# Attention: the exponentials of every third key tile are summed by accumulating transfers instead of VectorE adds

## The chip, the core and the metric

The kernel runs on one core of one Trainium2 chip. The core has five engines that run side by side, each with an instruction queue of its own that is worked off in order: TensorE (PE, matrix products), VectorE (DVE), ScalarE (ACT), GpSimd (POOL) and SyncE (SP, which only issues transfers). Transfers (DMAs) are issued by SP, by ScalarE, and in the changed kernel by GpSimd too; all run on the core's 16 DMA engines. The metric is the device time of one execution in microseconds; smaller is better.

## What is computed

One layer of a diffusion backbone over 2048 latent tokens with a prefix of 256 context tokens, d_model 1024, all in float32. The change touches the attention only:

```python
def attend(q, k, v):
    s = jnp.einsum('bkgqd,bknd->bkgqn', q, k, preferred_element_type=jnp.float32)
    p = jax.nn.softmax(s, axis=-1).astype(v.dtype)
    return jnp.einsum('bkgqn,bknd->bkgqd', p, v)
...
k_all = jnp.concatenate([k_c, k_x], axis=2)      # 256 context keys + 2048 latent keys
v_all = jnp.concatenate([v_c, v_x], axis=2)
attn_x = merge_heads(attend_blocked(q_x, k_all, v_all))
gm_x = gmlp_spatial(jax.nn.gelu(u_x), jax.nn.gelu(vg_x), gm_norm_g[l], gm_ws[l], gm_bs[l])
x = x + g1 * branch_merge(attn_x, gm_x, ga_x, gb_x, w_br_attn[l], w_br_gm[l], w_out[l])
h2 = modulate(x, norm2_g[l], sh2, sc2)
x = x + g2 * sq_relu_mlp(h2, w_ff1[l], w_ff2[l])
```

There are 8 query heads of 64 elements over 2 key/value heads. The softmax needs, for each query, the sum of the exponentials over all 2304 keys. That sum is the subject of the change.

## The kernel before

The kernel runs through four stages, one after the other: the input projections with norms and gates (to about 735 us), attention (about 735 to 1340 us), the merge of the branches with the output projection (to about 1700 us), and the MLP.

Attention is cut into 16 units: 4 query blocks of 512 queries, times 4 pairs of heads. A unit goes over the 2304 keys in 18 key tiles of 128 keys, two tiles in each of 9 cycles (`CYCLES`). The function `attend` writes out the order by hand. In cycle c of a unit stand, in this order:

- `maxima` (L2433), twice: TensorE computes scores of a coming unit once more (L2447) into one of three banks `m`, and VectorE reduces each bank to its maximum per query (L2457, L2452); the maxima later serve as the reference of the exponentials. Up to cycle 5 this is for the next unit, from cycle 6 on for the one after it.
- `scores` for the two key tiles of the cycle: TensorE computes them transposed, keys on partitions (L2504), with the reference added in the first two tiles by a product with `ones`; ScalarE takes the exponential of a whole 128x1024 tile (two heads of 512 queries, L2510). Tiles with an even number go to buffers `p2` (8 slots), those with an odd number to buffers `t4` (8 slots); the profile calls them `p` and `t`.
- `values` for the two tiles of the cycle before: TensorE multiplies them with v into the bank `o` (L2518).
- `gather` for the same two tiles: the exponentials are summed over the key tiles, elementwise, in two running sums. Key tiles 2, 5, 8, 11 and 14 (`ON_VECTOR`) go into VectorE's sum (L2535, one instruction of 128x1024 a tile); the other thirteen go into GpSimd's (L2538, two instructions of 128x512 a tile). The first tile of each sum is kept as it is, so VectorE has 4 adds in a unit and GpSimd 12 tiles, 24 adds. The running sums live in buffers `ac` (4 slots), two for each unit. The last unit has a list of its own (`LAST_ON_VECTOR`).
- `join` (L2549) for the unit before: VectorE adds its sum to GpSimd's (L2553), the first head in cycle 2 and the second in cycle 4. In cycle 5 `sums` (L2556) lets TensorE add up the 128 partitions of the result with a product by `ones`.
- other work in single cycles: in cycles 1 and 7 a step of the modulation weights on VectorE (L424, L428), in cycle 1 the inverse of the sums (L2579), in cycle 6 `reference` and `leading`, which turn the maxima of the next unit into rows and let SP write them into its tile `top` with eight small transfers (L2482); and in the last three to four units, in cycles 1, 4 and 7, a step of the next stage's inputs on VectorE (L1552, L1559).

The order within the queues of TensorE and VectorE is held as written (`self.fixed` in `build` and `order`). A slot of a buffer is taken again when its last reader has finished.

Of the kernel before, what the change touches and what calls it, by code (L numbers as in the profile page):

```python
# [14 lines left out]
ALU = mybir.AluOpType  # L15
# [54 lines left out]
PAIR = 2  # L70
CYCLES = NKT // PAIR
AHEAD = 6
ON_VECTOR = (2, 5, 8, 11, 14)
LAST_ON_VECTOR = (2, 4, 7, 8, 9, 12, 13, 14, 15)

OPENING = """
# [24 lines left out]
class Kern:  # L101
# [1324 lines left out]
    def attend(self, units, late, mod, key_loads):  # L1426
        self.psum({"s": 2, "m": 3, "o": 1})
        self.nc.gpsimd.memset(self.rg["q"], 0.0)
        begin = self.here()
        n = len(units)  # L1430
        pend = []

        def ordered(work):
            at = self.here()
            work()
            self.loads.append(range(at, self.here()))

        for i, u in enumerate(units):
            at = lambda k: units[k] if 0 <= k < n else None
            nxt, far, old, older = at(i + 1), at(i + 2), at(i - 1), at(i - 2)  # L1440
            u.banks()
            for c in range(CYCLES):
                step = nxt if c < AHEAD else far
                if c == 0 and far:
                    far.load()
                if step:
                    step.maxima(1)
                group = range(PAIR * c, PAIR * (c + 1))
                for j in group:
                    u.scores(j)  # L1450
                if step:
                    step.maxima(1)
                owner = u if c else old
                for j in pend:
                    owner.values(j)
                if c == 0:
                    if old:
                        old.leave()
                    u.o = self.bank([TB], tag="o")
                if c == 5 and old:  # L1460
                    old.sums()
                if c == AHEAD and nxt:
                    nxt.reference()
                    ordered(nxt.leading)
                for j in pend:
                    owner.gather(j)
                if i and c in (1, 7):
                    next(mod, None)
                if c == 1 and older:
                    older.inverse()  # L1470
                if c in (2, 4) and old:
                    old.join(c // 4)
                if i == 0:
                    next(key_loads, None)
                if i + c / CYCLES > n - 4 and c % 3 == 1:
                    ordered(lambda: next(late, None))
                pend = list(group)
        for _ in mod:
            pass
        owner = units[-1]  # L1480
        for j in pend:
            owner.values(j)
            owner.gather(j)
        units[-2].inverse()
        total = [self.sb("raw", [TB]) for _ in range(2)]
        for h in range(2):
            units[-1].join(h, total)
        self.fixed.append(range(begin, self.here()))
# [924 lines left out]
class Unit:  # L2413
# [109 lines left out]
    def gather(self, j):  # L2523
        k, nc = self.k, self.nc
        pt = self.pts.pop(j)
        e = j in (LAST_ON_VECTOR if self.last else ON_VECTOR)
        old = self.acc.get(e)
        if old is None:
            self.acc[e] = pt
            return  # L2530
        if e not in self.own:
            self.own.add(e)
            self.acc[e] = k.sb("ac", [2, TB])
        if e:
            nc.vector.tensor_tensor(out=self.acc[e], in0=old, in1=pt, op=ALU.add)  # L2535
        else:
            for h in range(2):
                nc.gpsimd.tensor_tensor(  # L2538
                    out=self.acc[e][:, h], in0=old[:, h], in1=pt[:, h], op=ALU.add
                )  # L2540
# [92 lines left out]
```

## Time and profile before

| | |
|---|---|
| median of 3 runs | 2974.29 us (2971.73 to 2974.46) |
| profiled execution | 2974.45 us, span of its instructions 2972.7 us |
| granted TensorE clock, mean | 0.993 |
| busy over the whole span: TensorE, VectorE, ScalarE, GpSimd | 98%, 69%, 47%, 21% |
| attention, 735 to 1340 us: TensorE, VectorE, ScalarE, GpSimd busy | 595.2, 509.7, 306.5, 554.0 us of 605 |
| DMA engines busy in attention, mean | 13% |

The shares of the whole span mix four stages: GpSimd has nearly all of its work in attention. In the rows of the profile, `ac<-ac,p` is an add of a `p` tile to a running sum, and "<-DVE ts L2457" behind a row means that the wait before it ended with that VectorE instruction. Rows of the form "start us, us, engine line op" come in order of time. Idle time of an engine costs nothing unless an engine that sets the end waits for it.

### The profile page before, as it was taken

What the parts mean: (1) busy time and instruction counts of PE and PEld (TensorE: products, weight loads), DVE (VectorE), ACT (ScalarE), POOL (GpSimd) and SP (SyncE); (2) the same over time, 40 slices, a digit from 0 to 9 for tenths busy, and PEclk for the clock granted to TensorE, in tenths of its full rate; (3) what the DMA queues carried; (4) which work ended last, traced back from release to release, by engine and by line L of the source; (5) the groups of instructions that cost most, each with busy time, mean ns of one, the idle gap of its engine ahead of it and who ended that gap; (6) DMA issues with size and microseconds to landing.
All of it is one profiled execution on the core that took longest, in us unless ns stands there. A gap on an engine that the chain in (4) does not pass through costs nothing. (4 is left out here: it accounts for less than half of the span.)

```text
span 2972.7 us, 39185 instructions
## 1 busy us (share of the span) xinstructions
PE 2898.6 (98%) x14126; PEld 2186.8 (74%) x14126; DVE 2058.5 (69%) x3018; ACT 1391.8 (47%) x1993; POOL 633.0 (21%) x444
## 2 busy tenths in 40 slices
PE   8999999999999999999999999999999999999999
PEld 7878787776554545447888878887888888888887
DVE  6866487766888898866555687775766766654555
ACT  6545865553554554553222354444453444444442
POOL 0000000000999999972221100000000000000000
PEclk9999999999999999999999999999999999999999
DMA  8688967777110100117766578888766444447654
GB/s 309 189 302 284 311 205 226 252 247 222 56 36 27 37 30 28 45 45 239 214 205 202 152 255 305 299 294 307 258 219 229 168 141 152 152 175 260 218 211 151
DMA packets 392947, 569.09 MB, mean 191 GB/s; under 512 B 39264, under 2 KB 194576, under 8 KB 392752
## 3 DMA queue, kind: packets, MB, share of 16 engines
q1 hardware_dynamic: 380448, 545.87, 54.8%
q10 hardware_dynamic: 12304, 20.71, 1.9%
q8 instruction: 111, 1.82, 0.3%
q14 instruction: 84, 0.69, 0.1%
HBM read 383.82 MB, written 182.58 MB: 191 GB/s over the span
## 5 line engine op out<-in xcount | busy, mean ns | idle before, releaser
L2457 DVE TENSOR_REDUCE ts<-m 128x1 f32<-128x512 f32 x472 | 300.2, 682 | 54.8 <-PE m L2447 52.8
L2061 DVE TENSOR_TENSOR b<-b,b 128x1024 fp32r<-128x1024 f32 x170 | 200.8, 1222 | 135.4 <-ACT b L2060 134.5
L2538 POOL TENSOR_TENSOR ac<-ac,p 128x512 f32<-128x512 f32 x160 | 266.3, 1686 | 42.7 <-ACT p L2510 42.5
L2060 ACT CAST b<-b 128x1024 fp32r<-128x1024 f32 x170 | 170.7, 1051 | 223.2 <-PE b L1945 100.1
L1944 PE MATMUL b<-b,b 128*128 128x512 f32 x680 | 265.1, 390 | 3.0 <-DVE b L2061 3.0
L1943 PE MATMUL b<-b,b 128*128 128x512 f32 x680 | 266.0, 391 | 1.7 <-DVE f L2082 1.5
L1945 PE MATMUL b<-b,b 128*128 128x512 f32 x680 | 264.7, 389 | 0.0
L2510 ACT ACTIVATE p<-s 128x1024 f32<-128x1024 f32 x149 | 152.4, 1026 | 223.7 <-PE s L2504 204.0
L2538 POOL TENSOR_TENSOR ac<-ac,t 128x512 f32<-128x512 f32 x184 | 251.3, 1393 | 6.1 <-ACT t L2510 6.1
L2504 PE MATMUL s<-h,h 64*128 64x512 f32 x1728 | 227.8, 391 | 0.0
L2504 PEld LDWEIGHTS s<-h,h 64*128 64x128 f32 x1728 | 161.3, 184 | 39.6 <-ACT t L2510 4.1
L1944 PE MATMUL b<-hb,b 128*128 128x512 f32 x446 | 174.1, 390 | 0.0
L1953 DVE TENSOR_TENSOR f<-f,b 128x512 f32<-128x512 f32 x160 | 109.3, 683 | 81.0 <-issue 46.9
L1945 PE MATMUL b<-hb,b 128*128 128x512 f32 x415 | 161.8, 391 | 0.0
L1943 PE MATMUL b<-hb,b 128*128 128x512 f32 x415 | 161.7, 390 | 0.0
L2518 PE MATMUL o<-p,h 128*64 128x512 f32 x596 | 160.8, 621 | 0.0
L1944 PEld LDWEIGHTS b<-b,b 128*128 128x128 f32 x680 | 127.7, 188 | 31.3 <-DVE b L2061 4.6
L1943 PEld LDWEIGHTS b<-b,b 128*128 128x128 f32 x680 | 127.6, 188 | 29.6 <-ACT b L2060 2.3
L2447 PEld LDWEIGHTS m<-h,h 64*128 64x128 f32 x584 | 60.4, 184 | 119.6 <-DVE ts L2457 95.9
L1945 PEld LDWEIGHTS b<-b,b 128*128 128x128 f32 x680 | 127.6, 188 | 26.4
L2518 PE MATMUL o<-t,h 128*64 128x512 f32 x556 | 144.7, 599 | 0.0
L2510 ACT ACTIVATE t<-s 128x1024 f32<-128x1024 f32 x139 | 141.4, 1018 | 0.0
(468 smaller groups left out, 7058.5 us busy)
## 6 DMA issues: line engine op xcount, KB each, us to landing
ao_d<-f SPq DMA_DIRECT2D x224, 256.0 KB
f<-in_w_ff SPq DMA_DIRECT2D x48, 1024.0 KB
b<-ao_d SPq DMA_DIRECT2D x85, 512.0 KB
b<-w2o_d SPq DMA_DIRECT2D x85, 512.0 KB
w2o_d<-f SPq DMA_DIRECT2D x112, 256.0 KB
f<-in_w_in SPq DMA_DIRECT2D x38, 512.0 KB
f<-x_d SPq DMA_DIRECT2D x64, 256.0 KB
hb<-ao_d SPq DMA_DIRECT2D x54, 256.0 KB
```

What stands on the lines that cost most here:

```text
L1943: mm(ps, wh, hh, start=start and k == 0, stop=False, skip_group_check=True)
L1944: mm(ps, wh, hl, start=False, stop=False, skip_group_check=True)
L1945: mm(ps, wl, hh, start=False, stop=k == len(w) - 1, skip_group_check=True)
L1953: nc.vector.tensor_tensor(out=out, in0=in0, in1=in1, op=op)
L2060: nc.scalar.copy(h, f32(l))
L2061: nc.vector.tensor_tensor(out=l, in0=f32(l), in1=f32(h), op=ALU.subtract)
L2447: nc.tensor.matmul(out, self.q[0][rows, tok], key[rows], start=True, stop=True)
L2457: nc.vector.tensor_reduce(out=self.mx[:, t, h, c : c + 1], in_=ps[h], axis=AX.X, op=ALU.max)
L2504: nc.tensor.matmul(s[:, h], w[rows], x[rows], start=j < PAIR and n == 0, stop=n == len(terms) - 1, skip_group_check=True,)
L2510: nc.scalar.activation(pt, s, AF.Exp)
L2518: nc.tensor.matmul(self.o[h * HD : (h + 1) * HD, :], k.V[c][:, i, self.kv * HD : (self.kv + 1) * HD], pt[:, h], start=j == 0, stop=j == NK ...
L2538: nc.gpsimd.tensor_tensor(out=self.acc[e][:, h], in0=old[:, h], in1=pt[:, h], op=ALU.add)
```

## The change

```diff
@@ -70,7 +70,7 @@
 AHEAD = 6
-ON_VECTOR = (2, 5, 8, 11, 14)
+SUMMED = 3
 LAST_ON_VECTOR = (2, 4, 7, 8, 9, 12, 13, 14, 15)
@@ -1468,8 +1468,8 @@
                 if c == 1 and older:
                     older.inverse()
-                if c in (2, 4) and old:
-                    old.join(c // 4)
+                if c in (3, 4) and old:
+                    old.join(c - 3)
@@ -2523,10 +2523,13 @@
         pt = self.pts.pop(j)
-        e = j in (LAST_ON_VECTOR if self.last else ON_VECTOR)
+        e = j in LAST_ON_VECTOR if self.last else j % SUMMED == SUMMED - 1
         old = self.acc.get(e)
         if old is None:
             self.acc[e] = pt
+            return
+        if e and not self.last:
+            nc.gpsimd.dma_start(out=old, in_=pt, accum_op=ALU.add)
             return
```

In each of the first 15 units, key tiles 2, 5, 8, 11, 14 and now 17 form the second sum. Tile 2's buffer is that sum, and tiles 5, 8, 11, 14 and 17 are added to it by five transfers from SBUF to SBUF that accumulate (each 128 rows of 4 KB, 512 KB). GpSimd issues them, in its own queue between its adds. GpSimd's own sum has one tile less (17). VectorE has no add of a key tile any more; it joins the two sums, in cycles 3 and 4 of the next unit instead of 2 and 4. Only one `ac` buffer is needed for a unit. The last unit stays as it was.

GpSimd's queue in the second unit, from key tile 3 on, before. `t_1398` is tile 3, `p_1407` tile 4, `p_1413` and `t_1414` are tiles 6 and 7, `t_1421` is tile 9; `Activation` is a wait for ScalarE, `Pool` one for GpSimd's own earlier work:

```order
L2538 TENSOR_TENSOR ac_7701<-ac_7701,t_1398_7689 128x512 [waits Activation_49,Pool_49]
L2538 TENSOR_TENSOR ac_7701<-ac_7701,t_1398_7689 128x512 [waits Pool_49]
L2538 TENSOR_TENSOR ac_7701<-ac_7701,p_1407_7722 128x512 [waits Activation_49,Pool_49]
L2538 TENSOR_TENSOR ac_7701<-ac_7701,p_1407_7722 128x512 [waits Pool_49]
L2538 TENSOR_TENSOR ac_7701<-ac_7701,p_1413_7757 128x512 [waits Activation_49,Pool_49]
L2538 TENSOR_TENSOR ac_7701<-ac_7701,p_1413_7757 128x512 [waits Pool_49]
L2538 TENSOR_TENSOR ac_7701<-ac_7701,t_1414_7765 128x512 [waits Activation_49,Pool_49]
L2538 TENSOR_TENSOR ac_7701<-ac_7701,t_1414_7765 128x512 [waits Pool_49]
L2538 TENSOR_TENSOR ac_7701<-ac_7701,t_1421_7801 128x512 [waits Activation_49,Pool_49]
L2538 TENSOR_TENSOR ac_7701<-ac_7701,t_1421_7801 128x512 [waits Pool_49]
```

The same place in the changed kernel (the numbers in the names differ, the tiles are the same; `p_1396` is tile 2, `t_1407` tile 5, `p_1418` tile 8; `DMASW` is a wait for an earlier transfer that GpSimd issued):

```order
L2541 TENSOR_TENSOR ac_7699<-ac_7699,t_1397_7687 128x512 [waits Activation_49,Pool_49]
L2541 TENSOR_TENSOR ac_7699<-ac_7699,t_1397_7687 128x512 [waits Pool_49]
L2541 TENSOR_TENSOR ac_7699<-ac_7699,p_1406_7720 128x512 [waits Activation_49,Pool_49]
L2541 TENSOR_TENSOR ac_7699<-ac_7699,p_1406_7720 128x512 [waits Pool_49]
L2532 DMA p_1396_7679<-t_1407_7728 128x1024 [waits PE_49,Activation_49]
L2541 TENSOR_TENSOR ac_7699<-ac_7699,p_1412_7754 128x512 [waits Activation_49,Pool_49]
L2541 TENSOR_TENSOR ac_7699<-ac_7699,p_1412_7754 128x512 [waits Pool_49]
L2541 TENSOR_TENSOR ac_7699<-ac_7699,t_1413_7762 128x512 [waits Activation_49,Pool_49]
L2541 TENSOR_TENSOR ac_7699<-ac_7699,t_1413_7762 128x512 [waits Pool_49]
L2532 DMA p_1396_7679<-p_1418_7790 128x1024 [waits DMASW5_49,Activation_49]
L2541 TENSOR_TENSOR ac_7699<-ac_7699,t_1419_7798 128x512 [waits Activation_49,Pool_49]
L2541 TENSOR_TENSOR ac_7699<-ac_7699,t_1419_7798 128x512 [waits Pool_49]
```

A transfer now stands after every two tiles of adds, and from the second on it waits for the one before it.

VectorE's queue around the two joins of a unit, before. `ac_8068` is GpSimd's sum and `ac_8145` VectorE's of the unit before; `p_1536` and `t_1546` are tiles 2 and 5 of the running unit, `m` the banks of the maxima:

```order
L2553 TENSOR_TENSOR ac_8068<-ac_8068,ac_8145 128x512 [waits DVE_49,Pool_49]
L2457 TENSOR_REDUCE ts_7991<-m_8476 128x1 [waits PE_49]
L2457 TENSOR_REDUCE ts_7991<-m_8477 128x1 [waits PE_49]
L2457 TENSOR_REDUCE ts_7991<-m_8498 128x1 [waits PE_49]
L2457 TENSOR_REDUCE ts_7991<-m_8499 128x1 [waits PE_49]
L2535 TENSOR_TENSOR ac_8510<-p_1536_8413,t_1546_8461 128x1024 [waits Activation_49]
L2457 TENSOR_REDUCE ts_7991<-m_8512 128x1 [waits PE_49]
L2457 TENSOR_REDUCE ts_7991<-m_8513 128x1 [waits PE_49]
L2457 TENSOR_REDUCE ts_7991<-m_8534 128x1 [waits PE_49]
L2457 TENSOR_REDUCE ts_7991<-m_8535 128x1 [waits PE_49]
L2553 TENSOR_TENSOR ac_8068<-ac_8068,ac_8145 128x512 [waits Pool_49]
```

And in the changed kernel, the same cycles (`p_1465` is tile 2 of the unit before, the sum of the transfers):

```order
L2457 TENSOR_REDUCE ts_7988<-m_8469 128x1 [waits PE_49]
L2457 TENSOR_REDUCE ts_7988<-m_8470 128x1 [waits PE_49]
L2457 TENSOR_REDUCE ts_7988<-m_8491 128x1 [waits PE_49]
L2457 TENSOR_REDUCE ts_7988<-m_8492 128x1 [waits PE_49]
L2556 TENSOR_TENSOR ac_8064<-ac_8064,p_1465_8044 128x512 [waits DMASW6_49,Pool_49]
L2457 TENSOR_REDUCE ts_7988<-m_8505 128x1 [waits PE_49]
L2457 TENSOR_REDUCE ts_7988<-m_8506 128x1 [waits PE_49]
L2457 TENSOR_REDUCE ts_7988<-m_8527 128x1 [waits PE_49]
L2457 TENSOR_REDUCE ts_7988<-m_8528 128x1 [waits PE_49]
L2556 TENSOR_TENSOR ac_8064<-ac_8064,p_1465_8044 128x512 [waits Pool_49]
```

The first join has moved down one cycle, to where the add of tiles 2 and 5 stood, and it waits for a transfer of GpSimd's as well as for GpSimd.

## The prediction

> **What bounds the kernel now.** I read the page first, for the share of each engine.
>
> ```profile
> span 2972.7 us, 39185 instructions
> ...
> PE 2898.6 (98%) x14126; PEld 2186.8 (74%) x14126; DVE 2058.5 (69%) x3018; ACT 1391.8 (47%) x1993; POOL 633.0 (21%) x444
> ```
>
> TensorE (PE) is busy for 98% of the span. These are averages over stages, and the change touches only attention, so next I read the busy time by stretches: attention as a whole, then single units (a unit is one query block and one pair of heads; its bounds here are the starts of the matmuls that put the maxima into a fresh pair of score banks).
>
> ```profile
> core 0: us, PE busy (x) PEld busy (x) DVE busy (x) ACT busy (x) POOL busy (x), PEclk, DMA share, GB/s
> 735.00:1340.00 605.00, 595.18 (x3615) 296.33 (x3612) 509.72 (x676) 306.52 (x345) 553.95 (x376) 0.99 0.13 41
> ...
> 843.78:880.75 36.97, 36.97 (x234) 18.75 (x231) 32.38 (x46) 18.90 (x21) 35.76 (x25) 1.00 0.11 34
> 880.75:917.72 36.97, 36.97 (x233) 18.68 (x231) 32.31 (x46) 18.90 (x21) 35.75 (x25) 1.00 0.11 37
> 917.72:957.18 39.46, 38.75 (x235) 19.20 (x232) 33.96 (x47) 18.89 (x21) 36.85 (x27) 1.00 0.11 36
> ...
> 1219.75:1260.39 40.64, 38.04 (x232) 19.00 (x230) 37.06 (x49) 20.54 (x24) 36.89 (x25) 1.00 0.15 46
> 1260.39:1304.26 43.87, 39.38 (x215) 17.74 (x211) 34.87 (x39) 20.44 (x24) 33.73 (x23) 0.92 0.08 26
> ```
>
> Attention takes 605 us, and TensorE idles for 9.8 of them. A regular unit (the first two unit rows) lasts 36.97 us with 36.97 us of TensorE in it: nothing to win there, whatever VectorE (DVE) does. GpSimd (POOL) is the next fullest, 35.76 of 36.97 us; VectorE has 32.4. The idle of TensorE sits in a few units late in the stage. The waits of TensorE over the same stretch (total, times, longest), the three longest of them, and VectorE's rows before the last of these say on what:
>
> ```profile
> PE m L2447 <- DVE ts L2457: 9.6, 8, 3.0
> ```
> ```profile
> 1257.76 0.50 PE L2447 MATMUL m<-h,h 64*128 64x512 f32 x1 [1.27 <-DVE ts L2457]
> ...
> 1271.93 0.50 PE L2447 MATMUL m<-h,h 64*128 64x512 f32 x1 [1.48 <-DVE ts L2457]
> ...
> 1288.82 0.50 PE L2447 MATMUL m<-h,h 64*128 64x512 f32 x1 [3.02 <-DVE ts L2457]
> ```
> ```profile
> 1283.13 1.67 DVE L2553 TENSOR_TENSOR ac<-ac,ac 128x512 f32<-128x512 f32 x1
> 1284.73 1.77 DVE L1552 TENSOR_TENSOR in<-raw,in 128x512 fp32r<-128x512 f32 x1
> 1286.42 1.75 DVE L1559 TENSOR_TENSOR raw<-in,gx 128x512 f32<-128x512 f32 x1
> 1288.09 2.47 DVE L2457 TENSOR_REDUCE ts<-m 128x1 f32<-128x512 f32 x4
> ...
> 1294.37 0.68 DVE L1552 TENSOR_TENSOR in<-raw,in 128x512 fp32r<-128x512 f32 x1
> ```
>
> All eight waits are for the reductions that empty the three banks of the maxima. In the longest (3.02 us), what stands before the reductions is a join (L2553) and the preparation of the next stage's inputs (L1552, L1559), not one of the adds that the change removes. The regular units have the same four adds and no wait at all. So the adds of VectorE lie beside TensorE's work and cost the span nothing now.
>
> **The change, step by step.** For each of 15 units (the last keeps its own list), four VectorE adds of 128x1024 go, GpSimd loses one key tile (17, two adds of 128x512), and GpSimd issues five transfers of 512 KB that add into key tile 2. The prices:
>
> ```profile
> L2538 POOL TENSOR_TENSOR ac<-ac,p 128x512 f32<-128x512 f32 x136 | 228.5, 1701 | 26.0 <-ACT p L2510 25.8
> L2538 POOL TENSOR_TENSOR ac<-ac,t 128x512 f32<-128x512 f32 x160 | 216.6, 1381 | 5.0 <-ACT t L2510 5.0
> ...
> L2535 DVE TENSOR_TENSOR ac<-ac,p 128x1024 f32<-128x1024 f32 x27 | 39.3, 1457 | 0.0
> ```
> ```profile
> L2538 POOL TENSOR_TENSOR ac<-ac,t x184: 1261/1277/2302, 739.9 to 1317.7; 128x512 f32<-128x512 f32 x184
> ```
> ```profile
> 846.38 2.52 POOL L2538 TENSOR_TENSOR ac<-ac,t 128x512 f32<-128x512 f32 x2
> ...
> 858.05 3.51 POOL L2538 TENSOR_TENSOR ac<-ac,p 128x512 f32<-128x512 f32 x2 [0.79 <-ACT p L2510]
> ...
> 858.99 1.42 DVE L2535 TENSOR_TENSOR ac<-p,t 128x1024 f32<-128x1024 f32 x1
> ```
>
> VectorE: 4 x 1.457 = 5.8 us fewer in a unit, 26.5 left of 36.97. This is off the path, so worth 0 directly. The join of the first half moves from cycle 2 to cycle 3, to the place in which an add stood; the join of the second half stays in cycle 4, so the longest wait above keeps all that stands before it.
>
> GpSimd: a pair of adds takes 2.52 us alone and 3.51 us next to a VectorE add, so each removed VectorE add gives GpSimd back 0.99 us. A unit is then 35.76 - 2 x 1.26 (tile 17) - 4 x 0.99 = 29.3 us of adds, and 36.97 - 29.3 = 7.7 us are left for five transfers: 1.54 us each. That is the point on which the forecast turns, because no row of the trace has GpSimd issuing a transfer. The nearest rows:
>
> ```profile
> L2547 ACTq DMA_DIRECT2D at_d<-t x15: 327/349/350, 774.4 to 1309.2; - x15
> ```
> ```profile
> 872.92 5.45 SPq L2482 DMA_DIRECT2D h<-t  x8
> 878.47 0.53 SPq L403 DMA_DIRECT2D raw<-in_w_mod  x1
> ```
>
> ScalarE's queue takes 0.35 us to issue a 128-row transfer, SP's 0.53 us; below that a gain is excluded, since an issue takes some time. The upper end is the time that GpSimd now needs for the same tile with arithmetic, 2 x 1.26 = 2.52 us. An issue handles 128 rows and not 131,072 elements, so I take a value nearer to the issue rows than to the adds, twice SP's and a little more: 1.2 us. Then GpSimd has 29.3 + 6.0 = 35.3 us in a unit of 36.97: hidden behind TensorE with 1.7 us to spare, about as full as today. If that cover goes, the excess is paid by TensorE, through the joins (rivals).
>
> The Trainium skill, "DMA: Bandwidth & Descriptors", section "Specifications", gives about 1 us to the first byte of a transfer issued by GpSimd against 0.6 for the other queues; section "SWDGE vs HWDGE vs iDMA" adds that only GpSimd can issue an accumulating one, because software there writes the descriptors. No row here shows either. Estimated from that page, GpSimd's sum would be 29.3 + 5.0 = 34.3 us, hidden as well.
>
> The transfer itself: each adds into the same tile, so GpSimd waits for transfer n to land before it issues n + 1, and the adds queued behind stand still. Between two of them are always two tiles, four adds, 4 x 1.26 = 5.0 us. The nearest row is a plain 256 KB store (issued at 1309.23; the columns are 0.2 us each from 1308):
>
> ```profile
> DMA  0000000000599800000000000000002389999999
> GB/s 0 0 0 0 0 0 0 0 0 0 215 379 399 307 10 0 0 0 0 0 0 0 0 0 0 0 0 0 0 0 84 118 251 315 346 282 300 325 364 241
> ```
> ```profile
> 1309.23 0.35 ACTq L2547 DMA_DIRECT2D at_d<-t  x1
> ```
>
> It starts 0.8 us after its issue and is through at 1310.8. 512 KB in one pass at 399 GB/s is 1.3 us; reading the target too and writing it back makes two to three passes, 2.6 to 3.9 us; with the start, 2.1 to 4.7 us. All of it is below 5.0, so this wait costs 0. I take 3.4 (two passes). Each further us would stop GpSimd four times a unit.
>
> The joins wait for the fifth transfer. Tile 17's adds now end at 848.9, 5.1 us after the unit's start at 843.78. The transfer, issued some 2 us earlier than that and 3 to 5 us long, lands 6 to 9 us after the start; the first join stands in cycle 3, about 15 us after it (a cycle is 36.97 / 9 = 4.1, and VectorE reaches the join at the end of its cycle). No wait, with some 6 us to spare. Key tile 2's buffer is now held until those joins instead of until the first add: seven of eight slots are left for one tile per cycle, 28 us ahead of their reuse, hidden. ScalarE's exponentials that reuse a tile read by a transfer now wait for its landing, 2 to 5 us later than an add's end, hidden by the same slots.
>
> What comes out for the span: a VectorE operation with two SBUF inputs takes 1.77 us next to GpSimd's adds and 0.68 us alone (both L1552 rows). GpSimd's adds cover 35.76 / 36.97 = 97% of a unit now and 29.3 / 36.97 = 79% then, so about 18% of TensorE's 9.8 us of idle should go by luck of position: 2 us. The profiled execution took 2974.45 us (span 2972.7), 0.16 us above the median of 2974.29; less 2 us that is 2972.
>
> **The rivals.**
>
> *GpSimd over its budget (slower).* If an issue takes longer than 1.54 us, every unit runs 5 x the excess behind. GpSimd's backlog first uses the 6 us ahead of the join; then VectorE waits in the join, its reductions stand behind, and TensorE waits for a bank. At 2.0 us: 5 x 0.46 x 15 - 6 = 28 us, 3002. At the upper end of 2.52: 5 x 0.98 x 15 - 6 = 67 us, 3041. For it: GpSimd is at 97% today, and software must handle two read rows for each written one. Against: it is freed of 6.5 us first, and all rows of an issue lie under 0.7 us. Chance 0.27.
>
> *The maxima's rows arrive late (slower).* SP issues the eight small transfers of the next unit's maxima from 872.92 to 878.37, and TensorE uses them here:
>
> ```profile
> 880.75 0.40 PE L2504 MATMUL s<-h,ones 64*128 64x512 f32 x2
> ```
>
> That leaves 2.4 us for the last one, which needs some 1.6 like the store above: 0.8 us to spare. The accumulating transfers of tiles 11 and 14 run at just that time on the same 16 DMA engines, which are now 11% busy. If they hold up the last row by more than 0.8 us, TensorE waits at each unit's start: with one whole transfer (2.6 us) in the way, 1.8 x 15 = 27 us, 3000; with half of it, 0.5 x 15 = 8 us, 2981. Against: pieces of 512 bytes slip in between the rows of a big transfer. Chance 0.11, together with a transfer that takes longer than the 5.0 us between two issues.
>
> *VectorE's relief shows after all (faster).* If GpSimd happens to be issuing or waiting, not adding, when L1552 and L1559 run, each of these takes 1.09 us less: the waits of 3.02, 1.5 and 1.3 us lose up to 2.2 each, the smaller ones about 1 us each, together some 8 us; and TensorE's clock (0.92 in the last unit row) keeps up, which is worth some 3 us more, since 8% of 43.87 us is 3.5. 2963. For it: GpSimd waits more, for ScalarE and for landings. Against: it catches up in the same cycles. Chance 0.18.
>
> **How the numbers follow.** Within 0.2% (6 us, about what can be told from no change) 0.44, the two slower cases 0.27 + 0.11 = 0.38, faster 0.18. The predicted time is that of no change, 2972. The range runs from the faster rival, 2963, to 3010, which takes in issues up to 2.15 us (5 x 0.61 x 15 - 6 = 40, less 2) and all of the late rows; beyond it are about a third of the slower cases and a quarter of the faster ones, 0.17. The likeliest case's own range is 2968 to 2978.
>
> **What would show it.** Right: regular units still 36.97 us; GpSimd's pairs at 2.5 us and no more at 3.5; four VectorE adds a unit gone; no wait of VectorE in the join; the waits of TensorE for reductions still near 9 us. Wrong: units of 38 us and more with GpSimd without idle time and joins that wait for GpSimd or a transfer (the first rival); TensorE waiting at the matmuls with `ones` (the second); issue time of more than 1.54 us, or landings more than 5 us after the issue.

## The result and the profile after

The changed kernel took 2991.44 us (median of 4 runs, 2990.17 to 2993.9) against 2973.38 us for the kernel before (4 runs, 2971.73 to 2974.46) on the same chip: a ratio of 1.006 [1.0048, 1.0072]. It is 18 us slower. The forecast was 2972 us, no change. The profiled execution took 2992.68 us, its span 2990.7 us. From the page, the span and the busy times of the engines, and the line of the new transfers out of `t` tiles (count, size, median time from issue to landing; 30 more come out of `p` tiles):

```profile
span 2990.7 us, 39205 instructions
...
PE 2905.3 (97%) x14126; PEld 2188.8 (73%) x14126; DVE 1976.0 (66%) x2958; ACT 1391.3 (47%) x1993; POOL 585.7 (20%) x489
...
p<-t POOLq DMA_DIRECT2D x45, 512.0 KB, 4.9
```

VectorE is 82 us and GpSimd 47 us less busy than before, as the change says, and the time is longer all the same: TensorE's work is the same, so it waits more. The busy times by stretches (same columns as in the prediction: attention as a whole, then single units):

```profile
735.00:1357.00 622.00, 601.76 (x3613) 296.86 (x3610) 426.55 (x615) 306.34 (x345) 507.21 (x421) 0.99 0.46 103
...
844.36:882.22 37.86, 37.57 (x232) 18.82 (x230) 27.35 (x41) 18.89 (x21) 32.51 (x28) 1.00 0.49 107
...
960.04:996.83 36.79, 36.79 (x233) 18.49 (x229) 27.20 (x41) 19.00 (x21) 30.79 (x27) 1.00 0.43 88
...
1225.12:1274.39 49.27, 42.35 (x234) 19.86 (x233) 36.09 (x44) 20.53 (x24) 33.91 (x29) 0.90 0.43 99
1274.39:1317.11 42.72, 38.10 (x215) 17.73 (x211) 27.80 (x34) 20.31 (x24) 28.95 (x25) 0.95 0.35 76
```

Two things are new. A regular unit (844.36) is 0.9 us longer than before, though the undisturbed one (960.04) is even 0.2 us shorter. And one unit in the last block, 40.64 us before, takes 49.27 us. GpSimd is busy for 32.5 us of a regular unit, adds and issues together, so it has room. TensorE's waits in attention point to two causes (total, times, longest):

```profile
PE m L2447 <- DVE ts L2457: 13.9, 8, 4.9
PE s L2504 <- DMA h<-t: 5.9, 7, 2.4
```

**First cause: the rows of the maxima come late.** The second line did not exist before. From the timeline, on TensorE the products with `ones` of a regular unit and of the last unit; on SP and on GpSimd what was under way before the last unit:

```profile
844.36 0.39 PE L2504 MATMUL s<-h,ones 64*128 64x512 f32 x1
845.04 0.47 PE L2504 MATMUL s<-h,ones 64*128 64x512 f32 x1 [0.29 <-DMA h<-t]
...
1317.11 0.50 PE L2504 MATMUL s<-h,ones 64*128 64x512 f32 x1
1320.02 0.76 PE L2504 MATMUL s<-h,ones 64*128 64x512 f32 x1 [2.41 <-DMA h<-t]
```
```profile
1310.92 5.91 SPq L2482 DMA_DIRECT2D h<-t  x8
```
```profile
1314.96 0.83 POOL L2532 DMA_DIRECT2D p<-p  x1
```

The rows of the first head are there, those of the second aren't. Tile 14's transfer (`p<-p` at 1314.96) is issued while SP issues the rows and lands after 4.5 us, at 1319.5; the second head's product starts at 1320.02. The other units show the same: in the three in which this transfer landed more than 2.2 us ahead of the unit's start, the second head's product was on time; in the other twelve it landed between 0.14 us ahead of the start and 2.4 us behind it, and the product was 0.4 to 2.9 us late.

From the first product with `ones` to the first matmul behind the block of scores a unit took 1.83 to 1.86 us before (2.37 in the last); now 1.84 to 3.38, and 6.26 in the last. The excess over the 15 units from the second on sums to 10.8 us. It is more than the 5.9 us of idle in the view, since a product that starts alone and its late partner run one behind the other instead of side by side; and about 1 us of the last unit's 3.9 is matmuls of 0.63 us instead of 0.39 behind the wait.

**Second cause: held VectorE operations.** In the unit from 1225.12, on VectorE, then on GpSimd, then on TensorE:

```profile
1245.02 1.19 DVE L2556 TENSOR_TENSOR ac<-ac,p 128x512 f32<-128x512 f32 x1
1246.14 5.85 DVE L1552 TENSOR_TENSOR in<-in,in 128x512 fp32r<-128x512 f32 x1
1251.91 2.47 DVE L2457 TENSOR_REDUCE ts<-m 128x1 f32<-128x512 f32 x4
```
```profile
1245.60 0.86 POOL L2532 DMA_DIRECT2D p<-p  x1
1246.21 2.79 POOL L2541 TENSOR_TENSOR ac<-ac,t 128x512 f32<-128x512 f32 x2
1248.68 2.74 POOL L2541 TENSOR_TENSOR ac<-ac,p 128x512 f32<-128x512 f32 x2
1251.11 1.18 POOL L2532 DMA_DIRECT2D p<-t  x1
```
```profile
1252.64 0.79 PE L2447 MATMUL m<-h,h 64*128 64x512 f32 x1 [4.95 <-DVE ts L2457]
1253.36 1.97 PE L2518 MATMUL o<-p,h 128*64 128x512 f32 x4
```

An operation that takes 0.68 us alone and took at most 1.79 us in the kernel before lasts 5.85 us, until GpSimd's four adds are over. The reductions stand behind it, TensorE waits 4.95 us for them, and its clock falls (0.90 in this unit). The unit is 8.6 us longer than before: 4.3 us more of idle (49.27 - 42.35 against 40.64 - 38.04) and 4.3 us more of busy time for the same work. Two more operations were held, for 3.38 and 3.46 us; TensorE waited 1.97 and 3.15 us behind them, where it had waited 1.27 and 3.02 before. From the second unit's start to the start of the merge it is 569.2 us before and 587.4 after, 18.2 more; 10.8 and 8.6 us are together a little more than that; the unit after the long one gives 1.2 back (42.72 us, 43.87 before).

### The profile page after: what moved, and what is told of

It reads as the page before. It is cut to its first block, busy times and chain, and to the rows that moved or that the text cites. A ratio compares the mean times of both kernels' runs of the same rounds, so it can differ in the third digit from the quotient of the medians.

```text
span 2990.7 us, 39205 instructions
## 1 busy us (share of the span) xinstructions
PE 2905.3 (97%) x14126; PEld 2188.8 (73%) x14126; DVE 1976.0 (66%) x2958; ACT 1391.3 (47%) x1993; POOL 585.7 (20%) x489
## 3 DMA queue, kind: packets, MB, share of 16 engines
q8 instruction: 111, 1.82, 0.3%
## 5 line engine op out<-in xcount | busy, mean ns | idle before, releaser
L2541 POOL TENSOR_TENSOR ac<-ac,p 128x512 f32<-128x512 f32 x160 | 217.0, 1426 | 51.4 <-ACT p L2510 51.2
L2541 POOL TENSOR_TENSOR ac<-ac,t 128x512 f32<-128x512 f32 x154 | 207.9, 1433 | 24.5 <-ACT t L2510 24.5
```

What stands on the lines that cost most here:

```text
L2541: nc.gpsimd.tensor_tensor(out=self.acc[e][:, h], in0=old[:, h], in1=pt[:, h], op=ALU.add)
```

## The experiments

Of the profiled executions, numbers named "first scores" and "unit" are counted as above, from the first product with `ones` of a unit.

**1. The second head's rows on another queue.** The changed kernel, with one edit in `leading`:

```diff
-                nc.sync.dma_start(
+                (nc.scalar if h else nc.sync).dma_start(
```

> The changed kernel, but the rows of the maxima's second head are written by ScalarE's queue instead of SP's, so that four transfers instead of eight stand in a row on SP. Theory of the late rows (the accumulating transfers hold up the last of the eight small ones, TensorE waits for them at each unit's start; summed over 15 units the first scores take 10.9 us more than before): the first scores of a unit are back at 1.84 us, and 8 to 11 us of the 18 lost are won back, about 2981 us. Theory of the held VectorE operation alone (one L1552 of 5.85 us in the unit at 1225): the first scores stay long or their time comes back elsewhere, 2988 to 2992 us. Theory that GpSimd is over its budget: no change, 2991 us.

Measured: 3001.74 us, ratio 1.0082 [1.0067, 1.0097]. First scores are at 1.84 us in nearly all units: the rows are on time, and the wait for them is gone. But the kernel got slower. TensorE's waits, and VectorE in a unit that takes 45.0 us here (40.3 in the changed kernel):

```profile
PE m L2447 <- DVE ts L2457: 19.7, 7, 5.0
PE s L2504 <- ACT p L2510: 6.4, 7, 2.7
```
```profile
955.34 0.69 DVE L456 TENSOR_TENSOR g<-m,g 128x512 f32<-128x512 f32 x1 [1.64 <-PE m L455]
956.06 5.28 DVE L458 TENSOR_SCALAR g<-g 128x512 f32<-128x512 f32 x1
```

Four units of 45 us stand here against one of 49 in the changed kernel. Other VectorE operations are now held (L458, in two units, is new), so which one is hit changes with a shift of some tenths of a microsecond; and ScalarE's issues delay exponentials. Curing one cause moved the other, and brought a cost of its own. The first scores came out as the first theory said; the time is outside all three forecasts.

**2. No transfers.** The five transfers of a unit are left out, so those tiles are missing from the sum, which is kept at 1 or more before the reciprocal:

```diff
         if e and not self.last:
-            nc.gpsimd.dma_start(out=old, in_=pt, accum_op=ALU.add)
+            pass
             return
```

> The changed kernel with the five transfers left out (tiles 5, 8, 11, 14, 17 are left out of the sum, and the sum is kept at 1 or more before its reciprocal). It shows what the rest of the change is worth, VectorE's adds gone and the joins moved. Both theories together: late rows gone and no GpSimd run that starts after an issue, so about the time before less the contention between VectorE and GpSimd, 2968 to 2974 us. If the move of the joins or the slots cost something by themselves: more than 2976 us.

Measured: 2974.31 us, 0.999 [0.9981, 0.9999]. The time is at the upper end of the first forecast. The wait for rows is gone and no operation is held. From the first unit's start to the merge it is 601.2 us here, 605.2 in the kernel before and 622.3 in the changed kernel: the rest of the change gains 4 us in these executions, and the transfers cost 21, of which the late first scores are 10.6 and the long unit (49.27 us, 40.50 here) 8.8. Everything that the change costs comes in with the transfers. One unit to keep in mind for later:

```profile
809.28:846.64 37.36, 37.36 (x232) 18.69 (x230) 28.29 (x41) 18.89 (x21) 29.79 (x23) 1.00 0.12 38
```

Units of 37.36 us appear without any transfer: where the last operation of the modulation weights in a unit (L428) starts together with an add of GpSimd, it lasts 1.85 us and the last reductions come late. In the next unit it lasts 0.87 us, and the unit 37.03; in the kernel before it lasts 1.58, and the unit 36.97.

**3. VectorE's adds again in the last block.** In units 12 to 14 the adds of tiles 5, 8, 11 and 14 are VectorE's, as before; transfers in units 0 to 11:

```diff
+        elif self.b == NB - 1:
+            e = j in ON_VECTOR
...
-        if e and not self.last:
+        if e and self.b < NB - 1:
             nc.gpsimd.dma_start(out=old, in_=pt, accum_op=ALU.add)
```

> The changed kernel, but units 12 to 14 (the last query block) sum tiles 2, 5, 8, 11, 14 on VectorE as before, without transfers; units 0 to 11 as changed. Theory of the held VectorE operation (L1552 and L1559 wait for a whole run of GpSimd's adds, when such a run starts after the issue of a transfer and just behind them): no L1552 or L1559 over 1.8 us, the unit at 1225 falls from 49.3 to about 41 us, and with the late rows of the last three units gone too 11 to 13 us are won back, about 2979 us. Theory of the late rows alone: only the 4.5 us of units 13 to 15 come back, 2986 us. GpSimd over its budget: 15 units of equal loss, so a fifth of 18 us, 2987 us.

Measured: 2985.12 us, 1.003 [1.0019, 1.004]. The waits (lines are one further down):

```profile
PE m L2448 <- DVE ts L2458: 11.1, 12, 2.0
PE s L2505 <- DMA h<-t: 2.9, 6, 1.2
```

No wait of 4.9 us is left, and the unit of 49 us is one of 41.8. About half of the loss is back. The late rows of the first twelve units stay. The ratio lies between the first theory's (2979 us of 2973 are 1.002) and the other two (1.0042 and 1.0046), so the time alone doesn't choose; the unit and the absence of held operations do. Experiment 9 bears on what is missing.

**4. Narrow transfers.** As many transfers, at the same places in GpSimd's queue, but of 64 columns (128 rows of 256 bytes); the rest of each tile is missing from the sum, kept at 1 or more:

```diff
-            nc.gpsimd.dma_start(out=old, in_=pt, accum_op=ALU.add)
+            nc.gpsimd.dma_start(out=old[:, 0, :64], in_=pt[:, 0, :64], accum_op=ALU.add)
```

> The changed kernel with transfers of the same 128 rows but only 64 of 1024 elements each (the rest of tiles 5, 8, 11, 14, 17 is left out of the sum, and the sum is kept at 1 or more before its reciprocal). GpSimd's issues stay, the traffic falls to a sixteenth. If the rows of the maxima are late because of the traffic on the DMA engines: the first scores are back at 1.84 to 1.9 us, and some 10 us come back, 2980 us. If they are late because of GpSimd's issuing: first scores as long as in the changed kernel, 2990 us. The held L1552 should stay in either case if it hangs on GpSimd's phase (issue, then adds), and go if it hangs on the data moved into SBUF.

Measured: 2985.1 us, 1.0028 [1.0018, 1.0039]. First scores are 1.84 to 1.86 us in all but the last two units. A regular unit, the disturbed one, and VectorE in it:

```profile
842.44:879.46 37.02, 37.02 (x232) 18.52 (x230) 27.37 (x41) 18.89 (x21) 32.52 (x28) 1.00 0.16 37
1220.23:1270.25 50.02, 42.11 (x232) 19.72 (x230) 37.29 (x45) 20.53 (x24) 33.31 (x29) 0.91 0.19 47
```
```profile
1242.00 5.85 DVE L1552 TENSOR_TENSOR in<-in,in 128x512 fp32r<-128x512 f32 x1
```

This separates the causes: without the traffic the rows are on time, and the hold stays to the hundredth. The late rows hang on the bytes, and the hold doesn't. The time is above the 2980 us expected, as the long unit is still there.

**5 and 6. Which transfer makes the rows late.** Experiment 3 again, with one tile more in GpSimd's own chain, tile 14 in the one and tile 5 in the other:

```diff
-            e = j % SUMMED == SUMMED - 1
+            e = j in (2, 5, 8, 11, 17)      # the other: (2, 8, 11, 14, 17)
```

> The third experiment again (last block's three units with the adds on VectorE, no transfers there), and in units 0 to 11 tile 14 goes to GpSimd's chain instead of a transfer: transfers of tiles 5, 8, 11 and 17 only. Theory (the rows of the maxima are held up by the transfer that is under way when they are written, that of tile 14): first scores back at 1.84 to 1.86 us in most units, wait of scores for the rows under 0.8 us in all (third experiment: 2.9), median 2 to 6 us below the third experiment's and ratio to before 0.999 to 1.001. Rival (the loss of the middle units lies in the number of transfers, wherever they stand): first scores between 1.86 and 2.4, a fifth less lateness than with all five, ratio 1.002 to 1.003. Second rival (GpSimd runs out: 1.0 us of issue goes, 2.5 us of adds comes, 34 of 37 us busy): VectorE's joins wait for GpSimd, units over 38 us, ratio over 1.005.

> The same, but it is tile 5 that goes to GpSimd's chain, and tiles 8, 11, 14 and 17 by transfer: the same number of transfers, of bytes and of GpSimd adds as in the kernel without tile 14's transfer. Theory (tile 14's transfer holds up the rows): first scores as late as in the third experiment (2.1 to 2.4 us where it is disturbed), the wait of scores for the rows about 2.9 us, ratio to before 1.002 to 1.004. Rival (the number of transfers counts): the same ratio as the kernel without tile 14's transfer, within 0.001.

Measured: 2983.66 us, 1.0036 [1.0017, 1.0054], without tile 14's transfer; 3022.56 us, 1.0162 [1.0148, 1.0176], without tile 5's. Products with `ones` and the waits of the first, then the waits of the second and its first unit:

```profile
L2505 PE MATMUL s<-h,ones 64*128 64x512 f32 x64 | 13.1, 393 | 0.0
```
```profile
PE m L2448 <- DVE ts L2458: 38.3, 15, 5.8
PE s L2505 <- DMA h<-t: 4.1, 6, 0.9
```
```profile
799.69 7.85 DVE L429 SCALAR_TENSOR_TENSOR raw<-raw,silu,raw 128x512 f32<-128x512 f32 x1
```

With the same number of transfers the rows are on time in the one (first scores at 1.83 to 1.87 us in all units but the last). In the other the second head's product is 0.8 to 1.3 us late in six of the twelve units behind transfers, and each of the other six follows a unit with a held operation. So the transfer under way while the rows are written makes them late, that of tile 14. The time expected for neither came out. The second was hit by six holds of 4.6 to 7.9 us, four of them on L429 (L428 in the changed kernel), which no run had held before. The first has no wait for rows and no hold in its last block (one of 3.13 us, on L425, near the start of attention) and is slower than expected all the same; experiment 9 bears on that.

**7. Gaps in GpSimd's adds, but no DMA.** Two copies of 32 numbers stand where the issue stood; the tiles are missing from the sum, kept at 1 or more:

```diff
-            nc.gpsimd.dma_start(out=old, in_=pt, accum_op=ALU.add)
+            nc.gpsimd.tensor_copy(out=k.gap, in_=f32(pt[:1, 0, :32]))
+            nc.gpsimd.tensor_copy(out=k.gap, in_=f32(pt[:1, 0, :32]))
```

> The changed kernel with each accumulating transfer replaced by two GpSimd copies of 32 numbers from the same tile (no DMA at all, so five tiles of six are left out of the third-tile sum; the sum is kept at 1 or more before the reciprocal). GpSimd's adds keep a short gap where the issue stood, and no traffic. Theory (the hold of a VectorE operation hangs on the phase: it starts in a gap, 0.1 us or less ahead of GpSimd's run of adds): VectorE operations of 3.3 to 5.9 us come back in the last block though no transfer is issued, first scores 1.84 to 1.86, ratio to before 1.002 to 1.004. Rival (the issue of the transfer itself brings it about): no VectorE two-input operation over 1.8 us, the unit from 1222 us 40.5 us long, ratio 0.999 to 1.000, as with the transfers left out. The copies last 0.2 to 0.5 us by the fixed part of small GpSimd operations; if their gap is much shorter than 0.47 us the run says less.

Measured: 2970.27 us, 0.9988 [0.9977, 0.9999]. Two held operations came, of 3.19 and 3.15 us, a little under the lengths expected, both L1560; VectorE and GpSimd around the first:

```profile
1257.05 3.19 DVE L1560 TENSOR_TENSOR raw<-in,gx 128x512 f32<-128x512 f32 x1
```
```profile
1256.63 0.56 POOL L2534 COPY gap<-p 1x32 f32<-1x32 f32 x1
1257.16 2.52 POOL L2543 TENSOR_TENSOR ac<-ac,t 128x512 f32<-128x512 f32 x2
```

So a hold needs neither a transfer nor its issue. The 5.85 us one did not come back, and the two cost next to nothing (units of 40.8 and 42.0 us, 40.5 and 41.8 in experiment 2); the expected ratio (1.002 to 1.004) was wrong.

**8. The control for ScalarE's queue.** The kernel before, with the edit of experiment 1.

> The kernel before, with the rows of the second head written from ScalarE's queue, as in the first experiment. Control: if ScalarE's eight issues a unit (0.5 to 0.6 us each) delay exponentials and with them the scores, this one loses too: 0.3 to 0.8 us a unit, ratio 1.002 to 1.004, and the first experiment's lack of a gain is put down to that. If not (ScalarE is idle 18 of 37 us a unit): ratio 0.999 to 1.001, and what the first experiment lost is put down to held VectorE operations alone.

Measured: 2977.88 us, 1.0014 [1.0005, 1.0023]; units of 37.3 to 37.9 us instead of 37.0. The issues on ScalarE cost about 4 us, which lies between the two forecasts (1.001 and 1.002). Of the other 20 us of experiment 1's loss, 17 are in its four units with a held operation (45.0, 45.0, 44.8 and 45.3 us against 39.5, 39.5, 40.6 and 43.9 before).

**9. The joins alone.** The kernel before, VectorE's adds and all, with the joins where the change puts them:

```diff
-                if c in (2, 4) and old:
-                    old.join(c // 4)
+                if c in (3, 4) and old:
+                    old.join(c - 3)
```

> The kernel before with one part of the change alone: the two joins in cycles 3 and 4 instead of 2 and 4; adds stay on VectorE. Theory (this part is worth nothing, as the kernel without transfers suggested): ratio 0.999 to 1.001, units of 36.97 us, no wait of a join. Rival (the join in cycle 3 pushes the reductions of that cycle: the matmuls of the maxima there came 0.3 us late in every kernel that has it): 0.1 to 0.3 us a unit, ratio 1.0005 to 1.0015.

Measured: 2992.45 us, 1.0069 [1.0057, 1.0082], far outside both. A regular unit, and VectorE and TensorE in its cycle 3:

```profile
846.27:884.65 38.38, 37.29 (x232) 18.75 (x230) 32.47 (x46) 18.90 (x21) 35.77 (x25) 1.00 0.11 33
```
```profile
861.49 1.41 DVE L2535 TENSOR_TENSOR ac<-p,t 128x1024 f32<-128x1024 f32 x1
862.82 1.78 DVE L2553 TENSOR_TENSOR ac<-ac,ac 128x512 f32<-128x512 f32 x1
864.53 2.47 DVE L2457 TENSOR_REDUCE ts<-m 128x1 f32<-128x512 f32 x4
```
```profile
865.26 0.49 PE L2447 MATMUL m<-h,h 64*128 64x512 f32 x1 [1.09 <-DVE ts L2457]
```

In cycle 3 the join meets the first add: 3.2 us of VectorE stand ahead of the reductions, and TensorE waits 1.09 us in this unit, 22.8 us in all of attention. VectorE's average of 85% says nothing of that. In the last block of experiments 3 and 5 VectorE's adds stand together with joins in cycles 3 and 4 too, so this probably is what they lacked; it wasn't tried by itself.

**10 and 11. The joins back in cycles 2 and 4**, with the transfers left out, and in the changed kernel (the edit of experiment 9 the other way round):

> The kernel with the transfers left out (tiles 5, 8, 11, 14 and 17 missing from the sum, which is kept at 1 or more before the reciprocal), and with the two joins back in cycles 2 and 4: so the kernel before without VectorE's four adds a unit, and nothing else. Theory by the last run (moving the joins alone cost 1.4 us a unit, so without the adds the move costs something too, and the adds are worth something): units of 36.5 to 36.8 us, 2 to 6 us in all, ratio 0.998 to 0.9993. Rival (the prediction's first step: with the joins in cycles 2 and 4 VectorE's adds are off the path and worth nothing, and what the moved joins cost came only from meeting an add in the same cycle): units of 36.9 to 37.0 us, ratio 0.9993 to 1.0005, the same as with the joins in cycles 3 and 4.

> The changed kernel with the two joins back in cycles 2 and 4; transfers as in the changed kernel. Theory (the loss is the late rows and the held operations): first scores as late as in the changed kernel (2.1 to 2.4 us in regular units), ratio between 1.002 and 1.007, according to which VectorE operations are held. Tile 17's transfer goes out in cycle 0 and takes 4.8 us, and cycle 2 begins some 8 us into the unit, so no join waits for it: if one does (a wait of VectorE for a transfer at the join, over 0.3 us a unit), the units get longer by as much, and the move of the joins was needed for the transfers. Rival (the place of the joins is what cost the 18 us, as it cost 20 us in the kernel before): ratio 0.999 to 1.001 in spite of late rows.

Measured: 2972.74 us, 0.9991 [0.9982, 1.0], without transfers (experiment 2: 0.999), and 2992.12 us, 1.0057 [1.0043, 1.0071], with them (the changed kernel: 1.006). The first ratio is in its theory's range, but the regular units took 37.1 to 37.4 us, which neither forecast had. Without VectorE's adds the place of the joins makes no difference that can be told. One join waits for a transfer, in the last unit, where VectorE has nothing else to do; and the same operation is held for 5.85 us. The joins are not the cause.

**12. The held operations moved.** In the changed kernel, the steps of the next stage's inputs one cycle later:

```diff
-                if i + c / CYCLES > n - 4 and c % 3 == 1:
+                if i + c / CYCLES > n - 4 and c % 3 == 2:
```

> The changed kernel with the steps that prepare the last matrix stage (the ones whose VectorE operations were held for 5.85, 3.38 and 3.46 us) taken one cycle later: cycles 2, 5 and 8 instead of 1, 4 and 7. Transfers, adds and rows as in the changed kernel. Theory (a hold is a matter of the moment at which the operation begins against GpSimd's run of adds): the three held operations don't come at these places; some are gone or of another length, the unit of 49.3 us falls to 40.5 to 44 us, and the kernel ends 2 to 8 us earlier than the changed kernel (ratio 1.003 to 1.0055), unless another operation is hit. Rival (any operation of this kind next to a transfer's issue is held): as many operations over 3 us, a unit of 49 us, ratio 1.006. The late rows of the maxima stay (about 10 us), so the ratio doesn't fall under 1.0025 by either.

Measured: 2975.81 us, 1.0016 [1.0007, 1.0025], below the range of the theory and below the 1.0025 that was called the floor. Waits, and the unit that had taken 49.27 us:

```profile
PE s L2504 <- DMA h<-t: 3.8, 6, 1.1
PE m L2447 <- DVE ts L2457: 3.1, 6, 0.6
```
```profile
1225.40:1263.27 37.87, 37.52 (x232) 18.61 (x231) 30.44 (x44) 20.02 (x23) 32.98 (x28) 1.00 0.47 106
```

The unit is 11.4 us shorter. Two operations are still held, for 3.11 and 3.35 us, at places where TensorE doesn't wait for them; the late first scores still cost 7.1 us.

**13 and 14. Both edits at once.** The changed kernel with tile 14 in GpSimd's chain (as in experiment 5, but in every unit that has transfers) and with the steps shifted (as in experiment 12); then the same with the joins in cycles 2 and 4:

> The changed kernel with two edits: tile 14 of every unit but the last goes to GpSimd's chain instead of a transfer, and the steps that prepare the last matrix stage come in cycles 2, 5 and 8. Theory (late rows and holds are the whole loss): first scores 1.84 to 1.86 us, no unit of 49 us, ratio 0.9985 to 1.001. Rival (a third cost of the transfers is left, such as the 0.35 us a unit seen with tile 14 on GpSimd): regular units of 37.3 to 37.4 us, ratio 1.0015 to 1.003.

> The same with the joins back in cycles 2 and 4. Theory: as in the run beside it within 0.001; beyond the 0.1% that leaving the transfers out brought there is nothing to win. Rival (VectorE's relief shows once nothing is late): ratio 0.996 to 0.998, units of 36.5 us.

Measured: 2970.99 us, 0.9995 [0.9981, 1.0009], and 2968.7 us, 0.9977 [0.9967, 0.9986]. First scores are at 1.83 to 1.86 us in all units but the last. Without the late rows and with those steps shifted the median is back at that of the kernel before. The two causes account for the loss; a smaller third cost isn't excluded, since the shift may bring a gain of its own (experiment 15). The regular units of 37.35 us are those of experiment 13's rival, but they come without transfers too (experiment 2). The first kernel still varies from 2964.65 to 2989.05 us; its profiled execution (span 2976.2 us) shows a reason, the second of two long holds (the other, of L424, lasted 5.93 us), on VectorE and on GpSimd:

```profile
991.58 8.11 DVE L428 SCALAR_TENSOR_TENSOR raw<-raw,silu,raw 128x512 f32<-128x512 f32 x1
```
```profile
991.60 2.68 POOL L2541 TENSOR_TENSOR ac<-ac,p 128x512 f32<-128x512 f32 x2
```

The second has no hold over 2.83 us and is the fastest kernel of this study, 6.9 us ahead of the kernel before: its ratio is the rival's, its units aren't (36.5 us). Two regular units and the two in the last block that were 40.64 and 43.87 us before:

```profile
841.28:878.64 37.36, 37.36 (x233) 18.70 (x230) 27.68 (x41) 18.89 (x21) 34.64 (x29) 1.00 0.41 93
878.64:916.00 37.36, 37.36 (x233) 18.72 (x230) 27.66 (x41) 18.89 (x21) 34.62 (x29) 1.00 0.41 94
1218.05:1255.86 37.81, 37.25 (x233) 18.52 (x230) 28.71 (x43) 20.01 (x23) 34.78 (x29) 1.00 0.41 95
1255.86:1297.52 41.66, 37.93 (x214) 17.62 (x211) 26.17 (x35) 20.82 (x25) 33.48 (x28) 0.96 0.40 87
```

The gain is in the last block, where VectorE has the most to do; the regular units are 0.4 us longer than before, by the effect seen in experiment 2, and not by the transfers.

**15. The shifted steps in the kernel before**, to see whether that gain belongs to the change.

> The kernel before with the steps that prepare the last matrix stage in cycles 2, 5 and 8 instead of 1, 4 and 7; adds and joins as before. Theory (the shift alone gives the 0.23%, since the gain of the version with four transfers lies in the last three units, 37.8 and 41.7 us against 40.6 and 43.9): ratio 0.9970 to 0.9985, last units some 2 to 3 us shorter each. Rival (the gain needs VectorE's adds gone): ratio 0.9992 to 1.0015, since VectorE's adds and joins meet the shifted operations in cycles 2 and 5.

Measured: 2974.1 us, 1.0004 [0.9995, 1.0013], as the rival said. By the medians the shift alone brings nothing, and the gain needs VectorE's adds gone. The profiled executions are less clear: the two units of the last block take 38.9 and 42.0 us here, and from the first unit's start to the merge it is 602.6 us, against 605.2 before and 599.5 in experiment 14, so part of the gain may be the shift's. Step by step, tile 14 on GpSimd took the ratio from 1.0016 (experiment 12) to 0.9995, and the joins back in cycles 2 and 4 to 0.9977, where the intervals still overlap. The shift without transfers, and with VectorE's adds gone, wasn't tried.

## Why the prediction was wrong, point by point

- *The adds of VectorE are worth nothing directly.* Held nearly: taking them out and nothing else was 0.9991 [0.9982, 1.0], 2.3 us. TensorE bounds a regular unit before and after.
- *GpSimd's budget*, on which the forecast was said to turn. Held. From the source view of the changed kernel (minimum, median, maximum of an issue in ns; landing in us):

```profile
L2532 POOL DMA_DIRECT2D p<-t x45: 852/1106/1206, 745.0 to 1320.5; - x45
L2532 POOL DMA_DIRECT2D p<-p x30: 826/860/1496, 752.7 to 1315.0; - x30
...
DMA to landing us min/median/max: 4.5/4.8/7.2
```

  An issue took 0.86 and 1.11 us at the medians and 1.50 at most, where 1.2 was taken and 1.54 was the limit. The sum of 35.3 us came out at 32.5: 4.8 for the five issues instead of 6.0, and 27.7 for the adds instead of 29.3. The first rival, with the second largest chance, didn't occur. The estimate by the Trainium skill's page "DMA: Bandwidth & Descriptors", section "Specifications" (34.3 us), which takes the page's 1 us to the first byte for the time of an issue, was a little nearer.
- *The transfer itself.* Taken 3.4 us, measured 4.8 at the median and 7.2 at most, over the upper bound of 4.7 that had been worked out. The median still stayed under the 5.0 us between two issues, and GpSimd waited for a landing once, for 1.3 us. This term of the sum was rightly near 0.
- *The joins.* No wait for a transfer, as forecast, and their new place costs nothing once the adds are gone. That it costs 20 us with the adds there (experiment 9) was not seen: the move was harmless only together with the rest of the change.
- *The rows of the maxima*: the step that failed first. It was named, with 0.8 us to spare and a price of 8 us if half a transfer stands in the way, and then given a chance of 0.11 on the argument that small pieces slip in between the rows of a big transfer. Here they came late: with 4.8 us from issue to landing in place of 3.4, tile 14's transfer was under way from the time of the second head's rows until about the unit's start, in 12 of 15 units. The price came out at 10.8 us. That it is near 8 is in part luck, since 3.9 of it fell in the last unit and 1.5 in the second; the chance was wrong. The page "DMA: Bandwidth & Descriptors" of the Trainium skill, section "Queues, rings and completion order", says that a DMA engine takes turns between queues by whole packets of some 9 to 17 descriptors. That agrees with rows that are late beside 4 KB rows and on time beside 256-byte ones, 5.9 against 0 us of waiting. No run shows the packets themselves, and the narrow transfers were also through sooner, 2.3 us after their issue, which would explain the same.
- *The last 2 us, from VectorE operations next to GpSimd's adds*: the step that failed with the wrong sign. It took 1.77 us as the price of an operation next to adds, about the longest such row of the kernel before, and let the price fall with GpSimd's share of the time. But that row was from queues in which VectorE's own adds stood and GpSimd's adds had no issues between them. With the transfers in GpSimd's queue one operation took 5.85 us and its unit 8.6 more. No row of the profile before showed it; a bound by the length of a run of adds (four, about 5 us) would have left room for it. The bound isn't the cause: why an operation is held stays open.
- *The third rival, VectorE's relief*: real in part, and hidden under the two losses. Without transfers it is 2.3 to 2.5 us by the medians; experiment 14, which also shifts steps and moves tile 14, comes to 6.9, where 11 were reckoned. Its mechanism shows little: seven of the twelve L1552 and L1559 still take 1.75 to 1.78 us in experiment 2, and eight took as much before.

The range (2963 to 3010) held the time, because the late rows and the slow issues had been given room in it. The slow issues, the larger part of that room, didn't occur, and the held operations had none, so that the time fell inside is partly luck.

## What to carry to other kernels

A small transfer that TensorE waits for can come too late beside a big one: look at what is in flight while it is written, and count the big one's whole time to landing against the spare time, not its share of the bandwidth. A price read from "next to" another engine holds for the order of the two queues that it was read from; where a change alters that order, allow for as much as the longest run of the other engine's work. And an edit that is harmless with another (the joins moved, with the adds gone) can cost 20 us without it (the joins moved, with the adds kept), so each part is to be tried alone before it is called free.

## What was not expected of the hardware

A VectorE operation on SBUF operands can be held until GpSimd's run of adds ends: 5.85 us for 0.68 us of work, up to 8.11 us. The 5.85, 3.38, 3.46 and 8.11 us operations all ended about 0.56 us after the last add of a run (of four, two, two and six behind their start). The Trainium skill, page "SBUF — State Buffer", section "Who interferes with whom", says that a VectorE instruction with two SBUF inputs contends with a GpSimd instruction that reads SBUF, which agrees with the 1.77 us rows; it also says that the issue order decides who blocks. The measurement differs there: L1552 began at 1246.14, 0.07 us ahead of GpSimd's add at 1246.21, and waited for four of them (start times on GpSimd are rough, so 0.07 us is not much to go by). What decides is open. Of 28 operations held for more than 3 us in the profiled executions, 19 began within 0.12 us of an add's start, but that is neither enough nor always needed: in experiment 13 six operations of L428 began 0.02 us ahead of an add, five of them took 1.83 to 1.85 us and one 8.11; and in experiment 6 three began in mid-add, up to 0.3 us ahead of an issue. In the kernels and blocks where VectorE has its own adds, none of L428, L1552 and L1559 took over 1.82 us. With neither VectorE's adds nor issues or copies in GpSimd's queue (experiments 2 and 10) none was held either.
